# Six up blocks instead of four by seven products, and weights handled in half units

## The chip, the cores and the metric

The kernel runs on one core of a Trainium2 chip. The metric is the device time of one execution in microseconds (us); the kernel before took 2269.77 us, the median of three runs from 2268.77 to 2270.17 us. The engines have these names in the profile: PE is the matrix engine (PEld its weight loads, which overlap PE), DVE the vector engine, ACT the scalar engine, POOL the general engine, and SP the engine whose queue issues the DMA loads.

## What is computed

A decoder trunk of two layers over x (256 tokens, 2048 channels, f32). Layer 0 mixes by differential attention, layer 1 by latent attention; each layer then attends to 256 memory tokens and ends in a dense MLP with squared ReLU. Every part is preceded by an RMS norm and added to the residual stream. The change lies in the MLP and in how weights are brought in for all parts:

```python
def sq_relu_mlp(h, wup, wdown):
    return jnp.square(jax.nn.relu(h @ wup)) @ wdown
...
for i in range(DEPTH):
    ...
    x = x + sq_relu_mlp(rms_norm(x, mlp_norm[i]), mlp_wup[i], mlp_wdown[i])
return rms_norm(x, final_norm)
```

wup is 2048 x 8192, wdown 8192 x 2048, for each of the two layers.

## The kernel before

**Three passes for one product.** Weights and activations are f32. Each is split into a high part, rounded to the matrix engine's f32r type, and a low part, the rest; a product is three matmuls (high by high, high by low, low by high; lines 184 to 198 in `unit_part`). So no weight goes to PE as it was loaded. A *unit* of weights is 512 rows by 512 columns, laid out as 128 partitions x 2048 f32 (1 MB). It is loaded into a raw tile by the SP queue (L168, `load`), and then split by halves of 128 x 1024: ACT casts the half to its high part `whi` (L196), and DVE subtracts it from the raw half to give the low part `wlo` (L197). Both lines stand in `split_pieces.next`. The pool `whalf` holds four halves of `whi` and four of `wlo`, so ACT can cast a half only when PE has finished the half four places earlier. The pool `wraw` holds six raw tiles of 1 MB (`RAWS = 6`).

**Order.** `plan` lists all units in the order in which PE takes them. `take` hands PE the next unit and lets `fill` write out instructions for up to four units ahead. The order of PE's instructions is the order of the program. The other engines' instructions are put in order by a scheduler when the program is built, with the loads held in program order. Side work (transposes, softmaxes, norms) runs as generators which `pump` steps between the matmuls when their due time on a counted clock has come.

**The MLP.** The 8192 hidden channels are eight blocks of 1024, each two halves of 512. An *up* block turns normalised x into 1024 hidden channels, and a *down* takes hidden channels back to 2048. An ordinary unit, of an up or a down, makes 24 matmuls of 512 columns (two halves, two row groups each, two token tiles of 128, three passes). An ordinary up block has eight units, so 192 matmuls.

Four of the eight blocks (`SEVEN = (1, 3, 5, 7)`) are computed by class `Seven` with seven products in place of eight (Strassen's scheme in Winograd's form): the activations are prepared once for the layer as sums and differences in class `Forms`, the weights' sums are formed on DVE while the weights come in (lines 742 to 763 in `Seven.job`), and the seven products are combined by DVE adds at the end (L789, in `Seven.products`). Each product has two units (x = 0 and 1), each with only 12 matmuls, as a product has one token tile only. That is 14 units and 168 matmuls for such a block. Products p5, p7, p6 and p4 need a weight sum for each of their units; p1, p3 and p2 do not. In PE's order a block is p1, p5, p1, p5, then p3, p7, p6, p2, p4 twice. Raw tiles are kept from one product to the next (`self.raw`), so that a block loads 12 units where an ordinary one loads 8.

`mlp_line` writes the order out by hand: block 0's eight units, then for each of blocks 1, 3, 5 and 7 its 14 units spread among the downs of the blocks before and the next ordinary up block (16, 24, 24 and 16 ordinary units), then block 7's down. A down's chunk covers one or two blocks and ends with two DVE adds into the residual (L442). When a hidden tile is complete, its task waits (`T_SQ` or `T_SQ + 4.0` on the counted clock), PE transposes it in groups of four (L162), and it is split again (L291 on ACT, L292 on DVE).

**Other uses of raw tiles.** `given_unit` (the first activations and the memory tokens), `prob_T`, `attend4`, `Forms` and the shared rotary key take whole raw tiles too, of which `given_unit`, `prob_T` and the rotary key use half.

**Start.** PE runs `WARM = 16` matmuls on a blank tile (L868), while the first weights come in by four loads of 256 KB on ACT's queue.

Of the kernel before, what the change touches and what calls it, by code (L numbers as in the profile page):

```python
# [10 lines left out]
F32 = mybir.dt.float32  # L11
# [6 lines left out]
P = 128  # L18
D = 2048
S = 256  # L20
# [3 lines left out]
WARM = 16  # L24
RAWS = 6
MLP_BLOCKS = 8
SEVEN = (1, 3, 5, 7)
# [18 lines left out]
def trunk(ctx, tc, x, xT, mem, memT, positions, gcols, gfinal, lam_vecs, consts, W, out):  # L46
# [9 lines left out]
    units = pool("units", 12)  # L56
# [12 lines left out]

    def half_unit():  # L70
        return units.tile([P, 2, 2, S], F32R, tag="half", name=nm("half"), bufs=2)
# [99 lines left out]
    stream = []  # L171

    def raw_tile():
        return wraw.tile([P, 4 * CH], F32, tag="raw", name=nm("raw"))

    def split_weights(src, width, pieces=2, loads=1, queue=None):
        raw = raw_tile()
        n = 4 * width
        m = n // loads
        for i in range(loads):  # L180
            load(raw[:, i * m : (i + 1) * m], src[:, i * m : (i + 1) * m], queue)
        return halves_of(raw, n, pieces)

    class split_pieces:
        def __init__(self, raw, n, pieces):
            self.raw, self.n, self.m, self.i = raw, n, n // pieces, 0
            self.halves = []

        def next(self):
            m, i = self.m, self.i  # L190
            at = i * m % (self.n // 2)
            if at == 0:
                self.halves.append([whalf.tile([P, 2 * CH], F32R, tag=tag, name=nm(tag)) for tag in ("whi", "wlo")])
            hi, lo = (w[:, at : at + m] for w in self.halves[-1])
            r = self.raw[:, i * m : (i + 1) * m]
            nc.scalar.copy(hi, r)  # L196
            nc.vector.tensor_tensor(lo, r, f32(hi), ALU.subtract)  # L197
            self.i += 1

    def halves_of(raw, n=4 * CH, pieces=2):  # L200
        split = split_pieces(raw, n, pieces)
        for _ in range(pieces):
            split.next()
        return split.halves
# [100 lines left out]
    def given_unit(src, u, gcol, pieces=None):  # L305
# [4 lines left out]
        for k, n in ((0, 1), (1, 1), (2, 2)) if pieces else ((0, 2), (2, 2)):  # L310
# [3 lines left out]
            for i in range(k, k + n):  # L314
                if pieces:
                    pieces.next()
# [54 lines left out]
    class Forms(Stream):  # L371
# [3 lines left out]
        def __init__(self, gcol):  # L375
            super().__init__(gcol)
            self.raw = [raw_tile().rearrange("p (k t) -> p k t", t=P) for _ in range(NT)]
# [13 lines left out]
        def feed(self, c, t, ps):  # L391
            xc = xs[t][:, c * CH : (c + 1) * CH]

            def task():
# [3 lines left out]
                rows = self.raw[t][:, 4 * c : 4 * c + 4]  # L398
# [7 lines left out]
        def sums(self):  # L406
# [3 lines left out]
            for x in range(2):  # L410
                a11, a12, a21, a22 = (self.raw[t][:, 8 * h + 4 * x : 8 * h + 4 * x + 4] for t in range(NT) for h in range(2))
# [100 lines left out]
    def prob_T(src, n, pt):  # L512
# [3 lines left out]
        o = raw_tile().bitcast(F32R)[:, : 2 * CH].rearrange("p (a c) -> p a c", a=2)  # L516
# [20 lines left out]
    def attend4(score_pairs, inputs, v, dst, causal):  # L537


        pTs = [raw_tile().bitcast(F32R).rearrange("p (a b c d) -> p a b c d", a=2, b=2, c=2) for _ in range(2)]  # L540

        def probs(t, heads, nk):
# [10 lines left out]
            for p in range(heads[0] // 2, heads[-1] // 2 + 1):  # L553
                at = (2 * p - heads[0]) * nb
                src = pt[:, at : at + 2 * nb].rearrange("p (h b) q -> p h b q", b=nb)
                hi = pTs[p][:, 0, :, :nb, t * P : (t + 1) * P]
                nc.scalar.copy(hi, src)
                nc.vector.tensor_tensor(pTs[p][:, 1, :, :nb, t * P : (t + 1) * P], src, f32(hi), ALU.subtract)
# [3 lines left out]
        def weighted(po, p, i, kb, passes, first, last):  # L562
# [3 lines left out]
            for j, (sv, sp) in enumerate(passes):  # L566
                mmul(
                    o, val(vt, sv, kb, (2 * p + i) * P, P), pTs[p][:, sp, i, kb, q],
# [137 lines left out]
    def plan_mlp(l):  # L706
        plan.extend(j for item in mlp_lines[l] for j in item.jobs)

    class Chunk:


        def __init__(self, l, kind, blocks, c):
            self.kind, self.blocks, self.c = kind, blocks, c
            if kind == "up":
                self.all = [(f"mlp_wup{l}", 4 * (2 * blocks[0] + c) + u, CH) for u in range(4)]
# [654 lines left out]
```

## Time and profile before

| | us | share of the span |
|---|---|---|
| median of three runs | 2269.77 | |
| the profiled execution | 2269.47 | |
| its span, first to last instruction | 2267.7 | 100% |
| PE busy | 2251.5 | 99% |
| DVE busy | 1609.2 | 71% |
| ACT busy | 1279.1 | 56% |
| POOL busy | 105.0 | 5% |

The DMA engines moved 458.90 MB, a mean of 202 GB/s over the span, and the clock granted to PE was 0.999 of full speed. The MLP of layer 0 has its units by seven products from 549 to 1134 us, that of layer 1 from 1613 to 2198 us. Numbers in the listings are microseconds from the span's start and microseconds of duration, unless marked ns. Successive instructions of one engine overlap a little in the records, so a run of them takes less than their durations added.

### The profile page before, as it was taken

The numbers are of one execution on the slowest core, as the hardware profiler recorded it, in microseconds if no ns is written. First come the engines' busy times: TensorE is split into PE (matmuls) and PEld (weight loads), VectorE is DVE, ScalarE is ACT, GpSimd is POOL, SyncE is SP. The second block draws the span as 40 slices with busy tenths as digits, with TensorE's granted clock in tenths as the row PEclk, the third lists the DMA queues.
The fourth block names the chain that finished last, engine by engine and source line by source line (L and its number), as shares of the span: only waits on it lengthen the run. The fifth ranks groups of instructions, "written<-read, shape, count | busy, mean of one in ns | idle before, by whom it ended". The sixth has DMA issues, their size and how long they took to land.

```text
span 2267.7 us, 27388 instructions
## 1 busy us (share of the span) xinstructions
PE 2251.5 (99%) x10668; PEld 1881.9 (83%) x10668; DVE 1609.2 (71%) x1766; ACT 1279.1 (56%) x1731; POOL 105.0 (5%) x194
## 2 busy tenths in 40 slices
PE   9999999999999999999999999999999999999998
PEld 7888888888888888888889888888888888888886
DVE  6665647777877776777865766778777776777775
ACT  6554545665565465455555655656556546546564
POOL 0211010000000000000000311000000000000001
PEclk9999999999999999999999999999999999999999
DMA  9436555436666656656655334644766666666672
GB/s 361 163 135 222 194 188 195 166 127 240 228 223 238 218 200 236 221 204 224 240 168 183 114 140 149 247 143 148 251 240 215 217 220 216 220 223 218 232 255 74
DMA packets 69969, 458.90 MB, mean 202 GB/s; under 512 B 8016, under 2 KB 8400, under 8 KB 17104
## 3 DMA queue, kind: packets, MB, share of 16 engines
q1 hardware_dynamic: 69264, 456.12, 57.2%
q8 instruction: 83, 1.36, 0.2%
q10 hardware_dynamic: 576, 1.05, 0.2%
q14 instruction: 46, 0.38, 0.0%
HBM read 455.04 MB, written 2.10 MB: 202 GB/s over the span
## 4 chain that ended last, share of the span: by engine, by line
PE 97%; DMA 1%; ACT 1%; DVE 1%; POOL 0%; issue 0%; ACTq 0%; POOLq 0%; SPq 0%
PE mm L158 77%; PE pr L158 13%; PE ax L158 3%; PE ax L162 2%; PE mm L162 1%; DMA raw<-in_da_wqkv_dram 1%; DVE wlo L197 0%; ACT whi L196 0%; DMA raw<-in_memT_dram 0%; ACT junk L325 0%; ACT ev L447 0%; POOL rope L458 0%; DVE unit L491 0%; DVE x L442 0%; ACT L918 0%
## 5 line engine op out<-in xcount | busy, mean ns | idle before, releaser
L158 PE MATMUL mm<-whi,unit 128*128 128x512 f32 (+1 forms) x5312 | 1681.4, 389 | 1.4 <-ACT unit L575 0.9
L197 DVE TENSOR_TENSOR wlo<-raw,whi 128x1024 fp32r<-128x1024 f32 (+2 forms) x890 | 1070.7, 1211 | 547.3 <-ACT whi L196 528.3
L196 ACT CAST whi<-raw 128x1024 fp32r<-128x1024 f32 (+2 forms) x890 | 925.6, 1040 | 849.1 <-PE mm L158 767.2
L158 PEld LDWEIGHTS mm<-whi,unit 128*128 128x128 f32 x5312 | 993.3, 188 | 197.9 <-ACT unit L575 1.3
L158 PE MATMUL mm<-wlo,unit 128*128 128x512 f32 (+1 forms) x2656 | 1025.1, 386 | 0.8 <-DVE wlo L197 0.8
L158 PEld LDWEIGHTS mm<-wlo,unit 128*128 128x128 f32 x2656 | 499.5, 188 | 94.4 <-DVE wlo L197 1.1
L158 PE MATMUL pr<-whi,unit 128*128 128x512 f32 x896 | 295.6, 390 | 0.0
L158 PEld LDWEIGHTS pr<-whi,unit 128*128 128x128 f32 x896 | 168.2, 188 | 34.8
L158 PE MATMUL pr<-wlo,unit 128*128 128x512 f32 x448 | 174.4, 389 | 0.0
L442 DVE TENSOR_TENSOR x<-x,mm 128x512 f32<-128x512 f32 x160 | 105.2, 681 | 8.6 <-PE mm L158 7.5
L158 PEld LDWEIGHTS pr<-wlo,unit 128*128 128x128 f32 x448 | 84.2, 188 | 17.2
L331 POOL TENSOR_TENSOR rs<-rs,mhalf 128x1 f32<-128x1 f32 (+1 forms) x28 | 24.6, 884 | 1271.4 <-DVE rs L330 1271.4
L292 DVE TENSOR_TENSOR unit<-ax,unit 128x512 fp32r<-128x512 f32 x80 | 54.1, 684 | 2.9 <-ACT unit L291 2.4
L291 ACT CAST unit<-ax 128x512 fp32r<-128x512 f32 x80 | 45.7, 582 | 10.5 <-PE ax L162 10.4
L504 ACT ACTIVATE p<-ax,nmax 128x256 f32<-128x256 f32 (+1 forms) x80 | 33.6, 428 | 31.1 <-DVE nmax L502 30.6
L757 DVE TENSOR_TENSOR raw<-raw,raw 128x2048 f32<-128x2048 f32 x16 | 36.6, 2289 | 9.2 <-DMA raw<-in_mlp_wup_dram 9.2
L325 ACT ACTIVATE junk<-x 128x512 bf16<-128x512 f32 x56 | 35.2, 628 | 9.4 <-DVE x L442 8.4
L1268 POOL TENSOR_TENSOR x<-x,unit 128x512 f32<-128x512 f32 x6 | 8.9, 1503 | 667.1 <-ACT junk L325 667.1
L749 DVE TENSOR_TENSOR raw<-raw,raw 128x2048 f32<-128x2048 f32 x16 | 36.6, 2286 | 2.3 <-DMA raw<-in_mlp_wup_dram 2.2
L754 DVE TENSOR_TENSOR raw<-raw,raw 128x2048 f32<-128x2048 f32 x16 | 36.6, 2285 | 0.9 <-DMA raw<-in_mlp_wup_dram 0.9
L158 PE MATMUL ax<-unit,unit 128*128 128x256 f32 (+1 forms) x240 | 37.2, 281 | 0.0
L762 DVE TENSOR_TENSOR raw<-raw,raw 128x2048 f32<-128x2048 f32 x16 | 36.7, 2291 | 0.6
(148 smaller groups left out, 1009.7 us busy)
## 6 DMA issues: line engine op xcount, KB each, us to landing
raw<-in_mlp_wup_dram SPq DMA_DIRECT2D x160, 1024.0 KB, 4.9
raw<-in_mlp_wdown_dram SPq DMA_DIRECT2D x128, 1024.0 KB, 4.9
raw<-in_da_wqkv_dram SPq DMA_DIRECT2D x47, 1024.0 KB, 5.6
raw<-in_da_wo_dram SPq DMA_DIRECT2D x16, 1024.0 KB, 5.0
raw<-in_ca_wkv_dram SPq DMA_DIRECT2D x16, 1024.0 KB, 4.9
raw<-in_mla_wo_dram SPq DMA_DIRECT2D x16, 1024.0 KB, 5.3
raw<-in_ca_wq_dram SPq DMA_DIRECT2D x8, 1024.0 KB, 4.9
raw<-in_ca_wo_dram SPq DMA_DIRECT2D x8, 1024.0 KB, 4.8
```

The source lines that it names most:

```text
L158: return nc.tensor.matmul(o, stationary, moving, start=start, stop=stop)
L162: nc.tensor.transpose(o, src, ident)
L196: nc.scalar.copy(hi, r)
L197: nc.vector.tensor_tensor(lo, r, f32(hi), ALU.subtract)
L291: nc.scalar.copy(hi, src)
L292: nc.vector.tensor_tensor(dst[:, 1, :n, t * P : (t + 1) * P], src, f32(hi), ALU.subtract)
L325: nc.scalar.activation(junk[:, : src.shape[1]], src, AF.Square, accum_out=acc)
L442: nc.vector.tensor_tensor(xc, xc, ps, ALU.add)
L749: nc.vector.tensor_tensor(o, o, r.pop("11"), ALU.subtract)
L754: nc.vector.tensor_tensor(o, r.pop("22"), o, ALU.subtract)
L757: nc.vector.tensor_tensor(o, r.pop("t3"), o, ALU.add)
L762: nc.vector.tensor_tensor(o, o, r.pop("21"), ALU.subtract)
```

## The change

- `SEVEN` becomes `(1, 2, 3, 5, 6, 7)`: six blocks by seven products, and blocks 0 and 4 the ordinary way, in each layer.
- `mlp_line` spreads the 84 units of those six blocks evenly over 64 ordinary units: k ordinary units are preceded by about 1.38 k of the others, until 61 are through. The two halves of block 4 are computed at two places, and go into the downs of blocks 1 and 3. There are now seven down passes over the 2048 output columns instead of five.
- A raw tile is 512 KB (128 x 1024) and there are 12 (`RAWS = 12`). Each unit is brought in by two loads, and sums of weights, casts and subtractions run by such halves. The users of raw tiles that needed a whole one take two, the others one.
- `WARM` is 13, `units` has 13 places while the two half-sized tiles of layer 1 are dropped, and the wait of the products' results on the counted clock is `T_SQ + 7.0`.

```diff
-WARM = 16
-RAWS = 6
+WARM = 13
+RAWS = 12
...
-SEVEN = (1, 3, 5, 7)
+SEVEN = (1, 2, 3, 5, 6, 7)
...
-    units = pool("units", 12)
+    units = pool("units", 13)
...
     def raw_tile():
-        return wraw.tile([P, 4 * CH], F32, tag="raw", name=nm("raw"))
...
+        return wraw.tile([P, 2 * CH], F32, tag="raw", name=nm("raw"))
+
+    def fetch(src, width=CH):
+
+        raws = [raw_tile()[:, : 2 * width] for _ in range(2)]
+        for h, raw in enumerate(raws):
+            load(raw, src[:, 2 * h * width : 2 * (h + 1) * width])
+        return raws
+
+    def half_tiles():
+        return [whalf.tile([P, 2 * CH], F32R, tag=tag, name=nm(tag)) for tag in ("whi", "wlo")]
+
+    def split_into(hi, lo, raw):
+        nc.scalar.copy(hi, raw)
+        nc.vector.tensor_tensor(lo, raw, f32(hi), ALU.subtract)
+
+    def split_half(raw):
+        hi, lo = (w[:, : raw.shape[-1]] for w in half_tiles())
+        split_into(hi, lo, raw)
+        return hi, lo
...
-                ready.append(split_weights(W[name][i, :, : 4 * width], width))
+                ready.append([split_half(raw) for raw in fetch(W[name][i, :, : 4 * width], width)])
...
                 elif p == "p7":
-                    r["t3"] = o = self.fetch(0, 1, x)
-                    nc.vector.tensor_tensor(o, r.pop("22"), o, ALU.subtract)
+                    r["t3"] = o = self.quarter(0, 1, x)
+                    other, args = r.pop("22"), lambda a, b: (b, a, ALU.subtract)
...
-                return halves_of(o)
+                    other, args = r.pop("21"), lambda a, b: (a, b, ALU.subtract)
+                halves = []
+                for h in range(2):
+                    if other is not None:
+                        nc.vector.tensor_tensor(o[h], *args(o[h], other[h]))
+                    halves.append(split_half(o[h]))
+                return halves
...
+        line = up(0, 0) + up(0, 1)
+        rest = (
+            down(*both(0)) + up(4, 0) + down(*both(1), (4, 0)) + down(*both(2))
+            + up(4, 1) + down(*both(3), (4, 1)) + down(*both(5)) + down(*both(6))
+        )
+        seven = [i for b in SEVEN for i in Seven(l, b).items()]
+        i = 0
+        for k, item in enumerate(rest):
+            while i < len(seven) and i * (len(rest) - 3) / len(seven) <= k:
+                line.append(seven[i])
+                i += 1
+            line.append(item)
+        return line, down(*both(7))
...
-    first = raw_tile()
-    for i in range(4):
-        load(first[:, i * CH : (i + 1) * CH], W["da_wqkv"][0][:, i * CH : (i + 1) * CH], nc.scalar)
+    first = [r[:, i * CH : (i + 1) * CH] for r in (raw_tile(), raw_tile()) for i in range(2)]
+    for i, raw in enumerate(first):
+        load(raw, W["da_wqkv"][0][:, i * CH : (i + 1) * CH], nc.scalar)
...
-            ready.append(split_weights(W["da_wqkv"][u], CH))
+            ready.append([split_half(raw) for raw in fetch(W["da_wqkv"][u])])
...
-                        lambda t, c, r, b=of.b: out(b, c, t, r, r, T_SQ + 4.0),
+                        lambda t, c, r, b=of.b: out(b, c, t, r, r, T_SQ + 7.0),
```

More of the change, by code (lines that the diff above doesn't have):

```diff
@@ L376, in __init__ @@
             super().__init__(gcol)
[L377 removed]
+            self.raw = [[raw_tile().rearrange("p (k t) -> p k t", t=P) for _ in range(2)] for _ in range(NT)]
             self.forms = {}
@@ L1056, in finish_chunk @@
                     r = work.tile([P, CH], F32, tag="ev", name=nm("ev"), bufs=EVS)
-                    out(of.blocks[0], of.c, t, ps[t], r, T_SQ)
+                    out(*of.halves[0], t, ps[t], r, T_SQ)
                 else:
@@ L1065, in acts_of @@
                 return [a.unit_of(u) for u in range(4)]
-            return [hid[b, c] for b in of.blocks for c in range(2)]
+            return [hid[k] for k in of.halves]
         def run(line, nxt=None):
@@ L1091, in run @@
                     finish_chunk(of, chunk["ps"], nxt)
-        line = mlp_lines[l]
-        tail = sum(len(i.of.all) == 2 and i.of.kind == "down" and i.of.blocks == [7] for i in line if not isinstance(i.of, Seven))
+        line, end = mlp_lines[l]
         limit = free_banks[0] - 1
         free_banks[0] -= limit
-        run(line[:-tail])
+        run(line)
         def last(nxt):
             free_banks[0] += limit
-            run(line[-tail:], nxt)
+            run(end, nxt)
         if gnext is None:
```

112 lines of the change are left out of this document (37 added, 75 removed).

## The prediction

> **What bounds the kernel now.** I read the page's busy times first, then the chain that ended last, then the groups of instructions with shapes kept apart, and last the MLP by stretches.
>
> ```profile
> span 2267.7 us, 27388 instructions
> PE 2251.5 (99%) x10668; PEld 1881.9 (83%) x10668; DVE 1609.2 (71%) x1766; ACT 1279.1 (56%) x1731; POOL 105.0 (5%) x194
> ...
> PE 97%; DMA 1%; ACT 1%; DVE 1%; POOL 0%; issue 0%; ACTq 0%; POOLq 0%; SPq 0%
> ```
>
> PE is 97% of the chain. Only removed matmuls, or its 16 us of idle time, can make the kernel faster, and anything that makes PE wait costs its full length. The stretch from the first to the last unit by seven products (columns: PE, PEld, DVE, ACT, POOL, granted clock, DMA share, GB/s) shows the other engines' room:
>
> ```profile
> 549.00:1134.00 585.00, 585.00 (x2635) 484.26 (x2634) 438.21 (x383) 330.16 (x359) 0.00 (x0) 1.00 0.64 224
> 1613.00:2198.00 585.00, 585.00 (x2635) 484.29 (x2634) 438.59 (x382) 330.02 (x359) 0.00 (x0) 1.00 0.64 224
> ...
> 1590.00:1600.00 10.00, 10.00 (x48) 8.26 (x47) 6.76 (x8) 6.61 (x10) 0.00 (x0) 1.00 1.02 411
> ```
>
> PE never stops there, at the full granted clock, with DVE at 75%, ACT at 56% and the DMA engines at 64%. So the question is what PE saves and whether DVE, the next in line, keeps up.
>
> **What PE saves.** Groups with shapes apart, and the chain in order of time:
>
> ```profile
> L158 PE MATMUL pr<-whi,unit 128*128 128x512 f32 x896 | 295.6, 390 | 0.0
> L158 PE MATMUL pr<-wlo,unit 128*128 128x512 f32 x448 | 174.4, 389 | 0.0
> ...
> 1097.82 2.72 PE pr L158 x12
> 1100.54 5.44 PE mm L158 x24
> ...
> 1126.38 0.44 PE ax L162 x4
> ```
>
> The records of 390 ns overlap, so the price of a matmul comes from the chain: 5.44 / 24 = 2.72 / 12 = 0.2267 us, the same for products (pr) and ordinary units (mm). The two pr rows hold 1344 matmuls, over eight blocks 168 each; an ordinary block has 8 x 24 = 192. Four blocks move (two a layer), so 4 x 24 = 96 matmuls go: 96 x 0.2267 = **21.8 us**. The number of transposes (four in 0.44 us) stays.
>
> **What DVE gains in work.** The prices, from groups and from DVE's order of time:
>
> ```profile
> L197 DVE TENSOR_TENSOR wlo<-raw,whi 128x1024 fp32r<-128x1024 f32 x854 | 1040.5, 1227 | 524.6 <-ACT whi L196 505.8 <-DMA memrow<-in_mem_dram 1.9
> L196 ACT CAST whi<-raw 128x1024 fp32r<-128x1024 f32 x854 | 898.9, 1053 | 820.3 <-PE mm L158 743.8 <-PE pr L158 56.3 <-DVE wlo L197 11.6
> L757 DVE TENSOR_TENSOR raw<-raw,raw 128x2048 f32<-128x2048 f32 x16 | 36.6, 2289 | 9.2 <-DMA raw<-in_mlp_wup_dram 9.2
> ...
> 571.17 3.49 DVE L197 TENSOR_TENSOR wlo<-raw,whi 128x1024 fp32r<-128x1024 f32 x3
> ...
> 596.28 2.29 DVE L762 TENSOR_TENSOR raw<-raw,raw 128x2048 f32<-128x2048 f32 x1
> 598.49 1.22 DVE L197 TENSOR_TENSOR wlo<-raw,whi 128x1024 fp32r<-128x1024 f32 x1
> ...
> L442 DVE TENSOR_TENSOR x<-x,mm 128x512 f32<-128x512 f32 x160 | 105.2, 681 | 8.6 <-PE mm L158 7.5
> ...
> 615.68 1.28 DVE L442 TENSOR_TENSOR x<-x,mm 128x512 f32<-128x512 f32 x2
> ```
>
> Instructions in a run follow each other more closely than they last: three subtractions take 3.49, so each holds DVE for (3.49 - 1.22) / 2 = 1.135 us; the next instruction starts 2.21 after a sum's start (I take 2.20); the second of two small ones comes 1.28 - 0.68 = 0.60 later. First I count the stretch before, to see whether such a count holds: 77 ordinary units and 56 of products give 266 halves x 1.135 = 301.9; 32 sums x 2.20 = 70.4; 92 small ones (32 adds of products, 30 residual adds, 30 splits of hidden tiles) x 0.60 = 55.2; together 427.5 against the 438.2 measured, 2.5% short. PE by the same count: 77 x 5.44 + 56 x 2.72 + 30 x 0.44 = 584.4 of 585.
>
> The stretch after has 61 ordinary units and 84 of products. PE: 61 x 5.44 + 84 x 2.72 + 30 x 0.44 = 573.5 us. DVE: 290 halves x 1.135 = 329.2. A sum of 128 x 1024 f32 does not occur before; its bounds are half of the 2289 ns row, 1.14, and the subtraction of the same shape, 1.23, and in a run I take 1.135: 48 sums by two halves are 109.0. Small ones: 48 adds, 46 residual adds (two more down passes) and 30 splits, 124 x 0.60 = 74.4. Together 512.6, with the 2.5% **525.4 us, 92% of PE's time**. DVE comes near, but PE stays the longer. ACT: 24 more casts x 1.05 and 4 copies, 330 + 27 of 573.5, 62%. DMA: four more loads of 1 MB for each moved block, 8 MB on 131 MB (585 us at 224 GB/s) in 573.5 us is 243 GB/s, 69%; the core reached 411 GB/s at 1590 us.
>
> By the Trainium skill (VectorE: DVE Perf Modes, "The DRAIN you can't avoid") the next instruction does not start until the pipeline has emptied, so that halves would pay a fixed part twice. The three subtractions in 3.49 disagree, each starting some 0.09 us before the last has ended. By the rule the sum would be 386 x 1.22 + 124 x 0.68 = 555 us, 97%, still under PE's.
>
> **Does 92% reach PE without stalls?** The densest part of a block is its last five products, with 3.6 ordinary units between them: PE 5 x 2.72 + 3.6 x 5.44 + 4 x 0.44 = 35.0 us. DVE has 17.2 halves and 6 half sums, 23.2 x 1.135 = 26.3, and 15 small ones, 9.0: 35.3 us. So there DVE is just full, and it enters that part with its lead; in the four units before (p1 and p5, with 2.9 ordinary ones) it has 21.7 us of work in 26.7. How large is the lead? The worst place I found before, in DVE's, ACT's and PE's order of time:
>
> ```profile
> 616.88 2.49 DVE L197 TENSOR_TENSOR wlo<-raw,whi 128x1024 fp32r<-128x1024 f32 x2
> 620.97 2.29 DVE L757 TENSOR_TENSOR raw<-raw,raw 128x2048 f32<-128x2048 f32 x1 [1.60 <-DMA raw<-in_mlp_wup_dram]
> 623.18 5.76 DVE L197 TENSOR_TENSOR wlo<-raw,whi 128x1024 fp32r<-128x1024 f32 x5
> 630.38 1.22 DVE L197 TENSOR_TENSOR wlo<-raw,whi 128x1024 fp32r<-128x1024 f32 x1 [1.44 <-ACT whi L196]
> ...
> 618.41 1.06 ACT L196 CAST whi<-raw 128x1024 fp32r<-128x1024 f32 x1 [0.30 <-PE pr L158]
> ...
> 625.24 0.39 PE L158 MATMUL pr<-wlo,unit 128*128 128x512 f32 x1
> ```
>
> A cast starts as soon as PE frees the `whi` of four halves earlier. The half cast at 618.41 could not be subtracted before 623.18, because p6's sum stood in front of it in DVE's order and waited 1.60 for its load; it was done at 624.40, and PE needed it at 625.24, 0.84 us later. DVE caught up within 8 us and idled again. After the change such a sum stands in the way for 1.135 instead of 2.20, and its first half needs only the first 512 KB:
>
> ```profile
> raw<-in_mlp_wup_dram SPq DMA_DIRECT2D x160, 1024.0 KB, 4.9
> raw<-in_mla_uq_rope_dram SPq DMA_DIRECT2D x4, 512.0 KB, 3.6
> ...
> SPq L168 <- DVE wlo L197: 1809.0, 382, 22.9
> ...
> DVE raw L757 <- DMA raw<-in_mlp_wup_dram: 9.2, 6, 2.1
> ...
> PE mm L158 <- DVE wlo L197: 0.8, 1, 0.8
> ```
>
> which lands 1.3 us sooner. The loads wait for raw places that DVE frees (the SP row); with halves a place comes free half a unit earlier. So the worst case gains 2.4 us of room, which the denser order takes back in part. There were 9.2 us of DVE waits at p6's 16 sums; its 24 sums would have 13.8, and the stalls of PE lie between 0 and that. Before, such waits cost PE nothing (its one wait for wlo, the last row, is at the start), and that is the nearest; I take 2 us.
>
> PE's other waits: a chunk's two banks must be emptied by L442 before the next chunk, and after the change a product unit of 2.72 us always lies between; the pair at 615.68 was done 1.3 us after it began.
>
> **The start.**
>
> ```profile
> 6.17 7.01 DMA raw<-in_da_wqkv_dram
> ...
> 6.70 0.51 ACT L318 ACTIVATE unit<-raw,g 128x256 fp32r<-128x256 f32 x1
> ...
> 14.30 0.50 PE L158 MATMUL mm<-whi,unit 128*128 128x512 f32 x1 [0.40 <-ACT whi L196]
> 15.56 0.50 PE L158 MATMUL mm<-wlo,unit 128*128 128x512 f32 x1 [0.76 <-DVE wlo L197]
> ...
> 60.71 0.66 PE L162 MATMUL mm<-identr,ev 128*128 128x128 f32 x4 [1.09 <-POOL ev L463]
> ...
> 6.31 0.15 PEld L868 LDWEIGHTS <-blank 128*128 128x128 bf16 x1 [0.28 <-issue]
> 6.74 0.40 PEld L868 LDWEIGHTS <-blank 128*128 128x128 bf16 x2 [0.28 <-issue]
> 7.25 0.19 PEld L158 LDWEIGHTS mm<-whi,unit 128*128 128x128 f32 x1
> ```
>
> The second unit of weights comes as two loads, and its first half can be split earlier, so the 1.16 us before 15.56 may go; but PE then reaches the rotary wait at 60.71 sooner, which may grow by as much. Three blank matmuls fewer: they run 0.43 us apart up to 6.74, so the thirteenth ends about 6.8, and the first real one starts after 7.2, which the first activations at 7.21 set (L318), not the blanks. The value I take is a gain of 0.6, between a gain of 1.2 and a loss of 1.6 (eight matmuls at 0.43 instead of 0.2267, if PE reaches full pace later).
>
> The Trainium skill (TensorE: Matmul & The Clock Gate, "What's actually happening") has the clock rise after some 3.4 us of sustained work in a free-running window. The blanks' change of pace between 6.3 and 7.2 agrees; thirteen blanks are still over 3.4 us, and by this rule, too, the loss could only be that 1.6.
>
> **The sum.** The profiled execution took 2269.47, its span plus 1.8 us around it, and stands 0.3 under the median. 2269.47 - 21.8 - 0.6 + 2 = 2249.1; I predict **2249 us**, its own range 2245 to 2254.
>
> **Rivals.**
>
> *Late loads reach PE.* The place at 620.97 was 0.84 us from a stall, and a DVE at 92% has less to catch up with. If at each of the 24 p6 sums 0.7 us came through (a wait of 1.5 us, which is 9.2 / 6, less 0.84), that is 17 us: 2264. Against it: loads by halves.
>
> *DVE becomes the bound through the order sum, cast, subtract (slower).* A summed half goes DVE, ACT, DVE. If the scheduler puts the subtraction right behind its sum in DVE's order, DVE stands still for the cast, 1.05 us, with everything queued behind it waiting, and PE after that. There are 96 such halves a layer, and DVE has 573.5 - 525.4 = 48 us to spare. It decides from 0.50 us a half, and outweighs the gain from (48 + 10.9) / 96 = 0.61, or 58% of the halves. At three quarters: 96 x 0.75 x 1.05 - 48 = 27.6 us a layer, 55 in all: 2303. For it: halves leave less of other work between. Against: in the rows above the subtraction after a sum starts 2.21 us after the sum's start, without a gap, as a half cast earlier was placed there.
>
> *The change does not save what it counts*, because product matmuls run slower when denser, or the first forms come late: 2269. The pr and mm pace is equal, and the first products stand where they stood.
>
> **Chances.** Forecast 0.60, late loads 0.16, DVE's order 0.20, no saving 0.04. About 0.2% either way (4.5 us) is what a measurement can tell from no change: faster 0.74, same 0.06 (no saving, and the upper edge of late loads), slower 0.20. The range, 2244 to 2269, leaves out DVE's order and takes in the others.
>
> **What would show it.** Right: 1344 and 672 pr matmuls in the whi and wlo groups; the stretch of the products near 574 us with PE busy throughout; DVE near 90% there; waits of PE for wlo no more than a few us in all. Wrong: rows of PE waiting for `wlo` that add up to over 10 us, or DVE idle before L197 right behind sums, or DMA waits of sums well over 14 us.

## The result, and the profile after

The changed kernel took 2292.53 us, the median of four runs (2286.72 to 2296.7), beside 2269.88 us for the kernel before (2268.77 to 2270.17). The ratio is 1.0099, with a 95% interval from 1.0083 to 1.0115: about 1% slower, where 1% faster was forecast. The profiled execution took 2286.72 us and is the fastest of the four.

The page of the kernel after, first its span and busy times, then the chain that ended last, then the DMA packets and SP's queue:

```profile
span 2284.9 us, 28887 instructions
PE 2240.1 (98%) x10569; PEld 1864.3 (82%) x10569; DVE 1763.5 (77%) x2002; ACT 1334.1 (58%) x1787; POOL 105.0 (5%) x194
...
DMA packets 136079, 475.83 MB, mean 208 GB/s; under 512 B 15360, under 2 KB 15744, under 8 KB 135808
...
q1 hardware_dynamic: 135360, 472.92, 62.9%
...
PE 78%; DVE 10%; DMA 9%; issue 2%; ACT 1%; POOL 0%; ACTq 0%; DVEq 0%; POOLq 0%
```

PE's share of the chain fell from 97% to 78%; DVE and the DMA engines now hold 19%. The span less PE's busy time is PE's idle time: 2267.7 - 2251.5 = 16.2 us before and 2284.9 - 2240.1 = 44.8 us after. So 28.6 us of new waits. PE's busy time fell by only 11.4 us, not by 21.8, so 10.4 us of it went elsewhere, up to 6.9 of them to the clock: its granted mean was 0.996, before 0.999, which is 2284.9 x 0.004 - 2267.7 x 0.001 = 6.9 us (an upper estimate, as PE stood idle in a part of the half-clock time; the rest isn't resolved). Together 28.6 + 10.4 = 39.0 us were lost against the saving of 21.8, and the span grew by 17.2.

Where this happened, by the matmuls of the products (number, shortest/median/longest in ns, start of the first and of the last). Kernel before, layer 0 and layer 1:

```profile
L158 PE MATMUL pr<-whi,unit x448: 389/389/481, 549.2 to 1133.8; 128*128 128x512 f32 x150
...
L158 PE MATMUL pr<-whi,unit x448: 389/389/481, 1613.1 to 2197.6; 128*128 128x512 f32 x150
```

Kernel after:

```profile
L155 PE MATMUL pr<-whi,unit x672: 387/389/628, 552.7 to 1147.2; 128*128 128x512 f32 x168
...
L155 PE MATMUL pr<-whi,unit x672: 387/389/481, 1627.1 to 2214.6; 128*128 128x512 f32 x168
```

The MLP of layer 0 begins 3.5 us late, so that much is lost at the start. It lasts 594.5 us instead of 584.6, and that of layer 1 587.5 instead of 584.5, where each was to become 11 us shorter. The groups and the waits for loads:

```profile
L155 PE MATMUL pr<-whi,unit 128*128 128x512 f32 x1344 | 439.5, 392 | 0.0
L753 DVE TENSOR_TENSOR raw<-raw,raw 128x1024 f32<-128x1024 f32 x192 | 233.0, 1222 | 78.7 <-DMA raw<-in_mlp_wup_dram 69.6
L155 PE MATMUL pr<-wlo,unit 128*128 128x512 f32 x672 | 263.8, 393 | 9.3 <-DVE wlo L184 9.2
...
raw<-in_mlp_wup_dram SPq DMA_DIRECT2D x352, 512.0 KB, 4.8
raw<-in_mlp_wdown_dram SPq DMA_DIRECT2D x256, 512.0 KB, 5.4
...
ACT whi L183 <- DMA raw<-in_mlp_wup_dram: 24.7, 19, 2.7
ACT whi L183 <- DMA raw<-in_mlp_wdown_dram: 15.3, 19, 1.7
```

The matmuls are as many as counted. The 512 KB loads land after 4.8 and 5.4 us, while the whole units before landed after 4.9. DVE's sums wait 69.6 us for loads, and ACT's casts 40 us. Before, the sums waited 12.3 us, 9.2 of them p6's. DVE took the 64 sums of before in program order; if it does so here, too, 35.3 of the 69.6 us stand at p6's sums and 22.7 at p7's, and 58.5 at first halves.

One stall in layer 0, in DVE's and PE's order of time (start, duration, idle before and what ended it):

```profile
899.40 1.23 DVE L753 TENSOR_TENSOR raw<-raw,raw 128x1024 f32<-128x1024 f32 x1 [0.52 <-DMA raw<-in_mlp_wup_dram]
...
902.40 1.23 DVE L753 TENSOR_TENSOR raw<-raw,raw 128x1024 f32<-128x1024 f32 x1 [0.65 <-DMA raw<-in_mlp_wup_dram]
903.55 3.49 DVE L184 TENSOR_TENSOR wlo<-raw,whi 128x1024 fp32r<-128x1024 f32 x3
908.74 1.23 DVE L753 TENSOR_TENSOR raw<-raw,raw 128x1024 f32<-128x1024 f32 x1 [1.71 <-DMA raw<-in_mlp_wup_dram]
...
911.60 1.23 DVE L753 TENSOR_TENSOR raw<-raw,raw 128x1024 f32<-128x1024 f32 x1 [0.50 <-DMA raw<-in_mlp_wup_dram]
...
913.88 0.68 DVE L277 TENSOR_TENSOR unit<-ax,unit 128x512 fp32r<-128x512 f32 x1
...
914.62 0.66 PE L159 MATMUL ax<-identr,ev 128*128 128x128 f32 x4 [1.99 <-DVE unit L277]
```

Four half sums in 13 us wait 3.4 us for their loads, and everything behind them on DVE moves back by as much: among it L277, which empties the bank that PE's next transposes need. PE stands still for 1.99 us. Then it pays again. The granted clock after that stall, by half microseconds (stretch, length, busy times, granted clock, DMA share, GB/s):

```profile
915.50:916.00 0.50, 0.50 (x3) 0.36 (x3) 0.50 (x2) 0.39 (x1) 0.00 (x0) 0.70 0.91 352
916.00:916.50 0.50, 0.50 (x3) 0.40 (x2) 0.50 (x1) 0.00 (x0) 0.00 (x0) 0.50 0.93 377
919.00:919.50 0.50, 0.50 (x4) 0.42 (x3) 0.50 (x1) 0.00 (x0) 0.00 (x0) 0.89 0.73 246
```

A mean of 0.70 in the first row is full clock until 915.7, one of 0.89 in the last is half clock until 919.1: 3.4 us at half clock, another 1.7 us lost. By the Trainium skill (TensorE: Matmul & The Clock Gate, "What's actually happening") the gate watches windows of some 3.4 us, and a whole idle one sets the clock back. The length agrees; the pause does not, as here one of 1.99 us did it (more on this in the last section).

### The profile page after: what moved, and what is told of

The parts are those of the page before. It is cut to its first block, busy times and chain, and to the rows that moved or that the text cites. A ratio compares the mean times of both kernels' runs of the same rounds, so it can differ in the third digit from the quotient of the medians.

```text
span 2284.9 us, 28887 instructions
## 1 busy us (share of the span) xinstructions
PE 2240.1 (98%) x10569; PEld 1864.3 (82%) x10569; DVE 1763.5 (77%) x2002; ACT 1334.1 (58%) x1787; POOL 105.0 (5%) x194
## 4 chain that ended last, share of the span: by engine, by line
PE 78%; DVE 10%; DMA 9%; issue 2%; ACT 1%; POOL 0%; ACTq 0%; DVEq 0%; POOLq 0%
PE mm L155 60%; PE pr L155 12%; DMA raw<-in_mlp_wup_dram 6%; DVE wlo L184 5%; PE ax L155 3%; DVE raw L753 2%; PE ax L159 2%; DMA raw<-in_mlp_wdown_dram 2%; PE mm L159 1%; ACT whi L183 1%; DVE x L427 1%; DMA raw<-in_da_wqkv_dram 1%; DVE unit L277 0%; DVE p L781 0%; DVE u L781 0%
## 5 line engine op out<-in xcount | busy, mean ns | idle before, releaser
L155 PE MATMUL mm<-whi,unit 128*128 128x512 f32 (+2 forms) x4800 | 1523.8, 389 | 10.2 <-DVE unit L277 4.9
L183 ACT CAST whi<-raw 128x1024 fp32r<-128x1024 f32 (+3 forms) x938 | 976.6, 1041 | 806.3 <-PE mm L155 634.7
L184 DVE TENSOR_TENSOR wlo<-raw,whi 128x1024 fp32r<-128x1024 f32 (+3 forms) x938 | 1121.0, 1211 | 353.9 <-ACT whi L183 331.8
L155 PEld LDWEIGHTS mm<-whi,unit 128*128 128x128 f32 x4800 | 898.4, 188 | 187.5 <-DVE unit L277 5.7
L155 PE MATMUL mm<-wlo,unit 128*128 128x512 f32 (+2 forms) x2400 | 927.7, 387 | 3.8 <-DVE wlo L184 3.7
L155 PE MATMUL pr<-whi,unit 128*128 128x512 f32 x1344 | 439.5, 392 | 0.0
L155 PEld LDWEIGHTS pr<-whi,unit 128*128 128x128 f32 x1344 | 253.2, 188 | 52.3
L753 DVE TENSOR_TENSOR raw<-raw,raw 128x1024 f32<-128x1024 f32 x192 | 233.0, 1222 | 78.7 <-DMA raw<-in_mlp_wup_dram 69.6
L155 PE MATMUL pr<-wlo,unit 128*128 128x512 f32 x672 | 263.8, 393 | 9.3 <-DVE wlo L184 9.2
L277 DVE TENSOR_TENSOR unit<-ax,unit 128x512 fp32r<-128x512 f32 (+1 forms) x88 | 57.4, 661 | 1.6 <-ACT unit L276 1.3
L155 PE MATMUL ax<-raw,unit 128*128 128x256 f32 (+1 forms) x240 | 35.3, 279 | 0.8 <-ACT unit L475 0.6
```

What stands on the lines that cost most here:

```text
L155: return nc.tensor.matmul(o, stationary, moving, start=start, stop=stop)
L183: nc.scalar.copy(hi, raw)
L184: nc.vector.tensor_tensor(lo, raw, f32(hi), ALU.subtract)
L277: nc.vector.tensor_tensor(dst[:, 1, :n, t * P : (t + 1) * P], src, f32(hi), ALU.subtract)
L753: nc.vector.tensor_tensor(o[h], *args(o[h], other[h]))
```

## The experiments

Two theories stood at first. The saving is there but **DVE is too full**: at some 90% of PE's time it can't catch up after a wait. Or **loading by halves** is what costs: the loads land too late. Each edit is against the changed kernel unless another is named. In thin_sums and whole_thin each weight sum is formed on 8 of its 1024 columns only; in half_bytes only the first half of every unit is loaded, and both halves are made from it.

**The whole loads back.** whole_six keeps the six blocks, their order, the half sums and the 13 blanks, but has six places of 1 MB and one load for each unit:

```diff
-RAWS = 12
+RAWS = 6
...
-        raws = [raw_tile()[:, : 2 * width] for _ in range(2)]
-        for h, raw in enumerate(raws):
-            load(raw, src[:, 2 * h * width : 2 * (h + 1) * width])
-        return raws
+        raw = raw_pair()[0]
+        load(raw[:, : 4 * width], src[:, : 4 * width])
+        return [raw[:, 2 * h * width : 2 * (h + 1) * width] for h in range(2)]
```

(`raw_pair` gives a tile of 1 MB and its two halves.) thin_sums and warm16 are the changed kernel with one line each, and halves_four is the changed kernel with the four blocks and the order of the kernel before:

```diff
-                        nc.vector.tensor_tensor(o[h], *args(o[h], other[h]))
+                        nc.vector.tensor_tensor(o[h][:, :8], *args(o[h][:, :8], other[h][:, :8]))
...
-WARM = 13
+WARM = 16
...
-SEVEN = (1, 2, 3, 5, 6, 7)
+SEVEN = (1, 3, 5, 7)
```

> Six blocks by seven products as in the change, but six raw places of 1 MB and one load of 1 MB for a unit, as before the change; sums and splits still by halves. Theory L (loads of 512 KB, with rows of 4 KB and twice the packets, are the trouble): DVE's waits for loads fall from 70 us to under 25, and the time to 2250 to 2262. Theory P (6 MB of raw places are too few for the denser order, whatever their size): places come free later than by halves, so as slow or slower, 2290 to 2315.

> The changed kernel with each weight sum formed for 8 of its 1024 columns only, so that raw places are held as long and loads are the same, and DVE is spared some 100 us of sums in each layer. Theory D (DVE's load of 92% is what makes PE wait): PE does not wait any more, 2248 to 2256. Theory P (late loads): DVE still waits for loads, though it catches up sooner; half of the loss or more stays, 2265 to 2285.

> The changed kernel with 16 blank matmuls at the start instead of 13. In the profile of the changed kernel the first real matmul starts at 10.13 us instead of 7.28, and runs 0.43 us apart until 14.6. Theory A (the blanks end at 5.7, PE stands idle 4.4 us and its clock falls back): the pace is full from the first matmuls on, and 2 to 3 us come back, 2289 to 2290. Theory B (the start is late because of the order on ACT alone): under 1 us comes back. Either way the some 35 us lost in the two MLP stretches stay.

> The change's handling by halves (12 places of 512 KB, loads, sums and splits by halves, 13 blanks) with before's four blocks in before's order. Theory L: the loads by halves cost here too, 2275 to 2285. Theory P: the order of before has room, so the time of before and the 3 us of the start, 2270 to 2274, with PE busy throughout the MLP.

Measured: whole_six 2262.79 us (ratio 0.9968, 0.9956 to 0.9980), thin_sums 2263.07 (0.9967, 0.9956 to 0.9979), warm16 2283.98 (1.0059, 1.0044 to 1.0074), halves_four 2308.9 (1.0169, 1.0153 to 1.0185). Both theories hold something: whole loads alone take back 30 us, and so does a DVE with free time. With four blocks the halves cost even more, 39 us, more than either theory had expected, and neither the order of six nor a full DVE is needed for that: in halves_four DVE is as busy as before (1609.8 us, 1609.2 before), and its sums wait 110.0 us for loads.

```profile
PE 2264.1 (98%) x10665; PEld 1883.6 (82%) x10665; DVE 1609.8 (70%) x1830; ACT 1281.1 (56%) x1731; POOL 104.9 (5%) x194
...
L753 DVE TENSOR_TENSOR raw<-raw,raw 128x1024 f32<-128x1024 f32 x128 | 155.5, 1223 | 114.5 <-DMA raw<-in_mlp_wup_dram 110.0
```

Why the halves cost more there than with six blocks was not tested. The page and the waits of whole_six:

```profile
PE 2235.2 (99%) x10569; PEld 1862.3 (82%) x10569; DVE 1765.0 (78%) x2002; ACT 1334.6 (59%) x1787; POOL 105.0 (5%) x194
...
raw<-in_mlp_wup_dram SPq DMA_DIRECT2D x176, 1024.0 KB, 4.8
raw<-in_mlp_wdown_dram SPq DMA_DIRECT2D x128, 1024.0 KB, 5.0
...
DVE raw L756 <- DMA raw<-in_mlp_wup_dram: 29.9, 30, 2.0
```

Twice the bytes land after about the same time. And thin_sums shows that late loads alone are not the whole of it:

```profile
L753 DVE TENSOR_TENSOR raw<-raw,raw 128x8 f32<-128x8 f32 x192 | 30.8, 165 | 152.1 <-DMA raw<-in_mlp_wup_dram 137.9
```

DVE waited 137.9 us for loads there, twice as long as in the changed kernel, and the time was 29 us better, which fits a DVE that has more room to wait (1576.2 us busy, 1763.5 in the changed kernel).

**Both at once, and four blocks with whole loads.** whole_thin is whole_six with thin sums; whole_four is whole_six with the four blocks and the order of before.

> The kernel whole_six (2262.8) with each weight sum formed for 8 of its 1024 columns: loads, places and holds are the same, DVE is spared about 100 us a layer. The prediction's sum without stalls is 2247. Theory D (the 15 us that whole_six lacks come from a DVE that is too full to catch up after a late load): 2246 to 2251. Theory P (late loads alone make PE wait): 2256 to 2263.

> Before's four blocks in before's order, with places and loads of 1 MB as before, but 13 blanks and weight sums by halves. If sums by halves and the rest of the change's edits are harmless, this is the time of before, 2268 to 2272; then the whole price of the halves in halves_four (2308.9) is that of places and loads of 512 KB. If sums by halves cost by themselves, 2273 or more.

Measured: 2248.07 us (0.9905, 0.9890 to 0.9920) and 2270.09 (1.0003, 0.9994 to 1.0013). whole_four is the kernel before in time, so half sums, half splits and the 13 blanks cost nothing as long as a unit comes as one load. whole_thin is what the prediction had worked out without stalls. Its page and its layer 0:

```profile
span 2245.7 us, 27571 instructions
PE 2229.0 (99%) x10569; PEld 1862.9 (83%) x10569; DVE 1585.7 (71%) x2002; ACT 1335.0 (59%) x1787; POOL 105.0 (5%) x194
...
L155 PE MATMUL pr<-whi,unit x672: 389/389/481, 548.8 to 1122.2; 128*128 128x512 f32 x168
```

PE's busy time is 22.5 us under that of before, its idle time 16.7 us as before, and the stretch lasts 573.4 us. The four kernels with six blocks make a square:

| six blocks, medians in us | thin sums | real sums |
|---|---|---|
| units by one load of 1 MB | 2248.1 | 2262.8 |
| units by two loads of 512 KB | 2263.1 | 2292.5 |

Real sums cost 14.7 us with whole loads, halves 15.0 us with thin sums, and both together 44.4: the last 14.7 are the one making the other worse.

**What of the halves costs it.** All three keep one 1 MB place for each unit. two_loads fills it by two loads; two_loads_rev issues them in the other order; rows_4k has one load, but a gap of 32 bytes between the halves of the place, so that every row of 8 KB is written as two of 4 KB (the room for it comes from the small tiles of statistics, which have one or two places fewer). Against whole_six, two_loads and rows_4k:

```diff
-        load(raw[:, : 4 * width], src[:, : 4 * width])
+        for h in range(2):
+            load(raw[:, 2 * h * width : 2 * (h + 1) * width], src[:, 2 * h * width : 2 * (h + 1) * width])
...
-        raw = wraw.tile([P, 4 * CH], F32, tag="raw", name=nm("raw"))
+        raw = wraw.tile([P, 2, 2 * CH + 8], F32, tag="raw", name=nm("raw"))
...
-        load(raw[:, : 4 * width], src[:, : 4 * width])
+        load(raw, src[:, : 4 * width].rearrange("p (h c) -> p h c", h=2))
```

> The kernel whole_six (six blocks, six places of 1 MB, 2262.8) with each unit brought in by two loads of 512 KB, one behind the other, into its one place. Theory S (small loads are the trouble, because each pays its own start and rows of 4 KB): back toward the changed kernel, 2280 to 2295. Theory G (the trouble lies in the places of 512 KB, each freed, waited for and filled by itself, so that the loads queue in another order): near whole_six, 2258 to 2268.

> The kernel two_loads (2278.6) with the two loads of a unit in the other order: the half that is used first lands last, so that DVE's and ACT's order can't count on an early first half; the number of loads, packets and places is the same. Theory O (the order planned for DVE and ACT counts on a first half that on the chip lands no sooner than a whole unit, and stands still for it): DVE's and ACT's waits for loads fall, and the time to 2264 to 2270, near rows_4k. Theory S (two loads cost by themselves, in landing time and packets): 2275 to 2285.

> The kernel whole_six with a gap of 32 bytes between the two halves of a place, so that the one load of 1 MB runs in rows of 4 KB and as many packets as in the changed kernel (some 135000 in all); a few small tiles have one buffer less. Theory R (it is the rows and packets): DMA share up from 58% to 62% and the time 2270 to 2290. Otherwise 2260 to 2268.

Measured: two_loads 2278.62 us (1.0040, 1.0025 to 1.0055), two_loads_rev 2277.17 (1.0041, 1.0026 to 1.0055), rows_4k 2267.66 (0.9992, 0.9982 to 1.0002). So the shorter rows, with the fewer small places, cost 4.9 us, the second load 10 to 11 more whichever half comes first, and the separate places, with the start that goes with them, the last 14. The start is a small part of these: the first product comes at 551.4 us in two_loads and at 552.7 in the changed kernel. The DMA rows of rows_4k:

```profile
q1 hardware_dynamic: 128272, 472.90, 59.2%
...
raw<-in_mlp_wup_dram SPq DMA_DIRECT2D x176, 1024.0 KB, 5.3
raw<-in_mlp_wdown_dram SPq DMA_DIRECT2D x128, 1024.0 KB, 5.5
```

and of two_loads, with its waits:

```profile
q1 hardware_dynamic: 135360, 472.92, 61.2%
...
raw<-in_mlp_wup_dram SPq DMA_DIRECT2D x352, 512.0 KB, 4.9
raw<-in_mlp_wdown_dram SPq DMA_DIRECT2D x256, 512.0 KB, 5.0
...
DVE raw L757 <- DMA raw<-in_mlp_wup_dram: 72.5, 55, 3.0
ACT whi L187 <- DMA raw<-in_mlp_wdown_dram: 24.5, 18, 1.7
ACT whi L187 <- DMA raw<-in_mlp_wup_dram: 11.8, 13, 1.7
```

Nearly twice the packets (whole_six has 71568) make a 1 MB load land 0.5 us later. Two loads bring back the waits of the changed kernel nearly in full. The issue and landing of each load stand in the traces, too (medians over the MLP's loads): two_loads issues a unit's second half 0.37 us behind the first; the first half lands after 4.2 us, 0.7 sooner than a unit of whole_six, and the second 5.6 us after the first was issued, 0.7 later. In the changed kernel the second half is issued 2.1 us behind the first, when its own place is free; the first lands after 5.1 us, the second 7.2 us after the first was issued.

**The order of the halves in the changed kernel, and the kernel once more.** halves_rev exchanges the two loads there (`for h in (1, 0)`); change_again is the changed kernel unaltered.

> The changed kernel (2292.5) with the same exchange of the two loads of each unit, 12 places of 512 KB as in the change. Theory O: 10 to 25 us come back, 2268 to 2282. Theory S: no change or slower, 2288 to 2300.

> The changed kernel once more, on the same chip as half_bytes, since its four runs were 10 us apart (2286.7 to 2296.7) where before's are 1.4 apart. If the spread comes with the chip: a narrower range elsewhere. If with the kernel (late loads land differently in each execution): again 5 to 15 us between runs, median 2284 to 2296.

Measured: 2284.58 us (2283.4 to 2288.2; 1.0070, 1.0055 to 1.0085) and 2290.5 (2289.2 to 2297.6; 1.0101, 1.0083 to 1.0119). The changed kernel's own runs spread over 10 us, and the exchange is worth 6 to 8 us, less than theory O expected and less than that spread; it isn't the main cause.

**What whole_six's last 15 us are.** Five edits of whole_six: one place less (places_5); the sums as one instruction of 128 x 2048 again (whole_sums_w16, beside whole_six_w16, both with 16 blanks); p4 ahead of p2, so that a raw tile is held for a shorter time (p4_first); half the bytes (half_bytes); and p4's sums on POOL (pool_p4).

```diff
-RAWS = 6
+RAWS = 5
...
-        ORDER = ("p1", "p5"), ("p3", "p7", "p6", "p2", "p4")
+        ORDER = ("p1", "p5"), ("p3", "p7", "p6", "p4", "p2")
...
-        load(raw[:, : 4 * width], src[:, : 4 * width])
+        load(raw[:, : 2 * width], src[:, : 2 * width])
...
-                        nc.vector.tensor_tensor(o[h], *args(o[h], other[h]))
+                        (nc.gpsimd if p == "p4" else nc.vector).tensor_tensor(o[h], *args(o[h], other[h]))
```

> The kernel whole_six with five raw places of 1 MB instead of six. Theory P (the time from a place coming free to its next use is what runs out, so that every load is as late as the places make it): the loads come a sixth earlier due, DVE's waits for loads rise from 30 us to over 100 and the time by 20 to 80 us, 2283 to 2340. If places are not short: under 5 us, 2260 to 2268.

> The kernel whole_six with 16 blank matmuls. If the short warm-up costs there what it did in the changed kernel (2292.5 to 2284.0, its profiled runs differ by 4 us at the first product and by more later), 2256 to 2260; if whole_six has no gap at its start, as its first product at 549.9 against 549.2 before suggests, no change, 2261 to 2264.

> The kernel whole_six with 16 blank matmuls and with each weight sum as one DVE instruction of 128 x 2048, as before the change. Theory: sums by halves help, since they stand in the way for half as long: this is slower than with halves by 2 to 10 us, 2262 to 2272. If halves of sums are only extra fixed cost (96 x 0.07 us a layer, 13 us of DVE time in all): the same or faster by up to 6, 2255 to 2262.

> The kernel whole_six with product p4 ahead of p2, so that t2 is held for one product less (some 6.7 us of a place, twice a block). Theory P: fewer late loads, DVE's waits fall from 30 us to 10 to 20 and the time to 2256 to 2261. Theory D: p6's six adds and p4's sum now fall closer together, no gain or a small loss, 2262 to 2266.

> The kernel whole_six (2262.8) with only the first 1024 of each unit's 2048 columns loaded, and both halves of the unit made from these: the same DVE, ACT and PE instructions, the same six places, one load of 512 KB for a unit in place of 1 MB, which should land in 3.6 us instead of 4.8. Theory L (how long a load takes to land is on the path, as each load starts only when DVE frees a place and the sums stand in DVE's order behind it): DVE's waits for loads go under 10 us and 6 to 13 us come back, 2249 to 2257. Theory D (a full DVE alone): 2260 to 2264.

> The kernel whole_six (2262.8) with product p4's weight sums on POOL, which is idle in the MLP; DVE is spared 24 half sums a layer, some 27 us. If a too full DVE is what whole_six's last 15 us come from, 4 to 9 us come back, 2254 to 2259. If POOL's sums are late (a sum of 128 x 512 took POOL 1.5 us, so some 3 us for a half) or slow DVE down, 2262 to 2275.

| kernel | median, us | ratio and interval |
|---|---|---|
| places_5 | 2262.74 | 0.9971 (0.9960 to 0.9982) |
| whole_six_w16 | 2262.88 | 0.9968 (0.9957 to 0.9979) |
| whole_sums_w16 | 2262.93 | 0.9970 (0.9959 to 0.9981) |
| p4_first | 2260.95 | 0.9965 (0.9952 to 0.9978) |
| half_bytes | 2260.26 | 0.9956 (0.9942 to 0.9971) |
| pool_p4 | 2283.5 | 1.0063 (1.0048 to 1.0078) |

One place less changes nothing, so places are not short (the sums even waited 13.8 us for loads instead of 29.9); nor do the halving of the sums or the blanks matter. The 1.8 us of p4_first are within the spread of its own runs (2260.3 to 2265.0), and its sums waited no less for loads (34.7 us). With half the bytes the loads land after 3.7 and 3.9 us, and the time moves by 2.5 us, though the sums' waits for loads rose to 52.8 us where theory L had them fall under 10; its stretch from 549 to 1134 us has PE busy for 578.77 us, whole_six's for 580.45, so the landing of a whole load is not it. Moving a quarter of the sums off DVE should then have helped. It made the kernel 21 us slower, more than was expected of late sums, and two rows of pool_p4 show where the gain went:

```profile
L756 POOL TENSOR_TENSOR raw<-raw,raw 128x1024 f32<-128x1024 f32 x48 | 148.6, 3106 | 1074.3 <-DVE wlo L187 1074.3
...
L187 DVE TENSOR_TENSOR wlo<-raw,whi 128x1024 fp32r<-128x1024 f32 x902 | 1146.0, 1291 | 346.8 <-ACT whi L186 334.8
```

A half sum takes 3.1 us on POOL, and DVE's subtractions, 1226 ns each in whole_six, took 1291 ns in the mean: 902 x 0.065 = 59 us more, as much as the 48 sums taken off DVE (48 x 1.22 = 59 us). They weren't all slowed alike. In the trace 46 of the 902, all beside a sum on POOL, took 1.85 to 3.44 us, and each ended 1.08 us after a sum on POOL had ended; the others stayed, but for eleven (ten in whole_six), at 1.3 us or less. So these 46 stood still until POOL was done. DVE got no emptier (1773.1 us busy, whole_six 1765.0), and PE's waits for `wlo` grew from 8.9 to 25.5 us.

**How steep it is.** whole_five is whole_six with five blocks by seven products, spread evenly over the ordinary units:

```diff
-SEVEN = (1, 2, 3, 5, 6, 7)
+SEVEN = (1, 2, 3, 5, 7)
...
+            down(*both(0)) + up(4, 0) + up(4, 1) + down(*both(1), *both(4)) + down(*both(2))
+            + up(6, 0) + down(*both(3)) + up(6, 1) + down(*both(6)) + down(*both(5))
```

> Whole places and loads as in whole_six, five blocks by seven products instead of six (block 6 the ordinary way again, the 70 units of the products spread evenly over 69 ordinary ones). PE's saving against before is 48 matmuls, 10.9 us, so without stalls 2258.9. DVE's work in the MLP lies half way, about 480 us of 579, 83%. If stalls come from a DVE that is too full to catch up, they set in steeply near the end: 2259 to 2263, 0 to 4 us of stalls, and PE waits below 12 us. If each added sum costs its own small stall, half of whole_six's 15 us: 2266. If the evenly spread order itself costs it, all 15: 2270 or more.

Measured: 2260.34 us (2260.08 to 2261.63; ratio 0.9960, 0.9946 to 0.9974). The stretch from 549 to 1134 us in whole_four, whole_five and whole_six, in that order (columns as in the prediction: PE, PEld, DVE, ACT, POOL, granted clock, DMA share, GB/s):

```profile
549.00:1134.00 585.00, 584.36 (x2629) 483.25 (x2629) 439.23 (x412) 329.24 (x357) 0.00 (x0) 1.00 0.64 224
```

```profile
549.00:1134.00 585.00, 584.35 (x2633) 483.30 (x2632) 485.26 (x465) 347.58 (x378) 0.00 (x0) 1.00 0.66 233
```

```profile
549.00:1134.00 585.00, 580.45 (x2601) 477.15 (x2600) 517.86 (x500) 360.56 (x391) 0.00 (x0) 1.00 0.66 240
```

With DVE at 439 of 585 us and at 485 (83%) PE hardly stops; at 518 (89%) it does. Against the time without stalls (2248.1 for six blocks, and 48 matmuls x 0.2267 = 10.9 more for five, 2259.0), five blocks lose 1.4 us and six 14.7. With whole loads that is steep, as a full DVE predicts; small stalls at every sum would have cost half. whole_five is the fastest complete kernel of the study, 0.4% under the kernel before, with p4_first 0.6 us behind it.

## Why the prediction was wrong, point by point

**The matmuls saved (21.8 us): right.** whole_thin's stretch lasts 573.4 us, 573.5 were worked out, and its 2248.07 us is the sum without stalls, 2269.47 - 21.8 - 0.6 = 2247.1, within 1 us.

**DVE's work: right.** The stretch of the changed kernel, from its first to its last product, in windows:

```profile
552.70:1147.20 594.50, 580.60 (x2580) 475.32 (x2580) 512.95 (x495) 355.94 (x386) 0.00 (x0) 0.99 0.71 234
```

512.95 us, and the count was 512.6; the 2.5% on top of it were too much. The 555 us by the Trainium skill's rule (VectorE: DVE Perf Modes, "The DRAIN you can't avoid") are not seen; that section itself lets an instruction that is not held start earlier.

**"In the way for 1.135 instead of 2.20, and its first half needs only the first 512 KB … which lands 1.3 us sooner": this step failed.** The 3.6 us came from four loads in another part of the kernel that do not come in pairs. A 512 KB load in the MLP took 4.8 and 5.4 us, as long as a whole unit's 4.9; half_bytes, with one such load for each unit, has the short landing (3.7), two_loads has 4.9 and 5.0. The time rose with what was on its way beside it: in the changed kernel a half landed after 3.7 us when none of the MLP's other loads was on its way as it was issued, 4.5 with one, 5.2 with two and 6.0 with three (medians), and on average two were (before, 0.6 of the whole units). So the first half landed 5.1 us after its issue, no sooner than a whole unit, and the "2.4 us of room" for the worst case lack these 1.3. That sums by halves stand in the way for less is true and was worth nothing (whole_sums_w16 equals whole_six_w16). All in all loads and places by halves cost 2292.5 - 2262.8 = 30 us; how much of it came through the late first halves isn't separated.

**"I take 2 us", stalls between 0 and 13.8: the mis-sized term.** With whole loads it is 14.7 us, just beyond the upper bound. The bound scaled the sums' waits of before (9.2 us) by their number, 24 for 16. But what reaches PE doesn't go by the waits' number or sum: half_bytes' sums waited 52.8 us and places_5's 13.8, and the two are 2.5 us apart. The prediction had found that DVE is "just full" in the last five products of a block, 35.3 us of work in 35.0, and then took the lead it enters with to be enough, from a kernel where it always had caught up.

**The start: wrong in sign.** 0.6 us were to be gained, 3.5 were lost. ACT's order of time at the start of the changed kernel, then PE's:

```profile
9.05 0.62 ACT L183 CAST whi<-raw 128x512 fp32r<-128x512 f32 x1 [2.88 <-DMA raw<-in_da_wqkv_dram]
9.58 0.50 ACT L303 ACTIVATE unit<-raw,g 128x256 fp32r<-128x256 f32 x1
```

```profile
1.22 4.50 PE L866 MATMUL ax<-blank 128*128 128x512 bf16 x13 [1.22 <-DVE coef L928]
10.13 0.80 PE L155 MATMUL mm<-whi,unit 128*128 128x512 f32 x1 [4.41 <-ACT unit L303]
```

The first activations, at 6.70 before, stand at 9.58 on ACT behind the cast of the third quarter of weights, which waits for its load. So they did set the first real matmul, as the prediction said, but the prediction had not asked what would stand ahead of them. The 13 blanks, spent at 5.72, let PE idle for 4.41 us and begin at half clock. The prediction had them end at about 6.8, by the pace of before; in this execution the full pace came earlier, at 4.3 us. With 16 blanks (warm16) the kernel took 8.5 us less, of which some 4 lie at the start (its first product matmul comes at 548.9 us); the rest is near the kernel's own spread. In whole_six the blanks make no difference, and in whole_four, whole_thin and whole_five, also with 13, the first product comes at 548.6 to 548.9 us, a little earlier than before (549.2).

**The rivals.** "Late loads reach PE" is what happened, though only half of the sums' waits stand at p6 (35.3 of 69.6 us, by the order above), and "against it: loads by halves" was upside down. That its 2264 us is near whole_six's 2262.8 is luck, as it priced p6's sums alone. "DVE's order sum, cast, subtract" is not what made it slower: with whole loads sums by halves and whole took the same time, and in the changed kernel DVE's subtractions waited less for casts than before (331.8 us, 528.3 before, all shapes). What would have warned was named: waits of the sums well over 14 us (69.6 came), and PE's waits for `wlo` (9.2 and 3.7 us).

**Still open.** Why a second load costs 10 to 11 us beyond its packets, where the places are the same and the order of the halves makes no difference; how the last 14 us divide between the separate places, the start and the order of DVE's instructions, which is made anew for every kernel and was not held fixed; and why loads by halves cost more with four blocks than with six.

## What to carry to other kernels

With whole loads DVE hid its waits when it was 83% busy and did not at 89%: a forecast that fills an engine further needs the stalls priced where its work is densest, not scaled from the emptier kernel. A share of busy time is no guarantee, though: in halves_four's products DVE was 73% busy (436.9 of 602.6 us), and late loads reached PE all the same. Halving a transfer brought its first half 0.7 us sooner or not at all, where a lone load of that size promised 1.3; take the landing time from loads issued in the same pattern, with as many others on the way. When a change bundles a saving with a new way of loading, test the two apart, as here the saving was real and the way of loading ate it twice over.

## What the runs showed of the hardware

A pause of PE of 1.99 us was followed by 3.4 us at half clock, and one of 1.82 us (up to 1003.85) likewise, while four others in the same execution, of 2.11 to 2.60 us, were not. Where the pause falls matters: the clock fell at 7.75, 915.70 and 1004.44 us, which are 266 and 26 times 3.413 us apart, so the falls lie on a grid of that step. Both pauses lay whole within one step (from 912.28 and from 1001.03 us), with PE busy for 1.43 and 1.59 us of its 3.41; each of the four others is cut in two by the grid. One of these still left a step (from 1984.07) with PE busy for only 1.50 us, and the clock did not fall, so the exact measure isn't settled.

Rows of 4 KB instead of 8 KB let a 1 MB load land 0.5 us later. A 512 KB load landed after 3.7 us alone and after 6.0 with three others on the way. POOL's f32 sums of 128 x 1024 took 3.1 us against DVE's 1.22, and 46 of DVE's 902 subtractions stood still for them, up to 3.44 us long instead of 1.22.
